# Two small tables placed ahead of hT in on-chip memory, so that hT starts at 192 modulo 512 bytes

## The chip, the core and the metric

The kernel runs on one core of a Trainium2 chip. The core has a matrix engine (TensorE, "PE" in the profile, with its weight loads as "PEld"), a vector engine (VectorE, DVE), a scalar engine (ScalarE, ACT), a general engine (GpSimd, POOL) and a queue that issues transfers (SyncE, SP). Operands lie in on-chip memory of 128 partitions (SBUF); matrix products land in PSUM, a separate memory.

The metric is the device time of one launch in microseconds, the median of several runs. Lower is better.

## What is computed

One layer of a hybrid decoder block on 512 tokens of width 1024, in float32. A single input projection is split into the inputs of a state-space branch, of a dilated attention branch, and of two gates:

```python
h = rms_norm(x, norm_w[layer])
proj = h @ w_in[layer].astype(f32)                 # (512, 1024) @ (1024, 9216)
u_s, z_s, q, k, v, z_a, r_s, r_a = jnp.split(proj, offsets, axis=-1)
y_s = s5_branch(u_s, ...)                          # state-space scan, GELU, GLU with w_glu
y_s = (y_s * jax.nn.silu(z_s)) @ w_ssm_out[layer]
q, k = rms_norm(q, ...), rms_norm(k, ...)          # per head, then partial rotary
y_a = dilated_attention(q, k, v)                   # 3 groups of 8 heads, windows 128/512/2048
y_a = (y_a * jax.nn.silu(z_a)) @ w_attn_out[layer]
m = jax.nn.sigmoid(r_s) * y_s + jax.nn.sigmoid(r_a) * y_a
x = x + m @ w_o[layer]
```

The projection `h @ w_in` is by far the largest product: 9216 of the columns, against 1024 each for `w_glu`, `w_ssm_out`, `w_attn_out` (half as deep) and `w_o`.

## The kernel before, in words

**Split products.** Every float32 operand of a large product is held as two tiles of a reduced float32 format, a high part and a low remainder, and `mm3` (line 122) multiplies hi by hi, hi by lo and lo by hi into the same PSUM bank. So one logical product of a 128-deep slice is three matmuls. In the profile all of these have line L63, the helper that issues a matmul, and are told apart by their tiles: `pj<-hT_hi,w_lo` is a product into the PSUM tile `pj` from `hT_hi` and `w_lo`.

**hT.** The normed input is transposed once, at the start, into `hT_hi` and `hT_lo` (line 220 and 221 allocate them, 250 and 251 write them): 8 slices of 128 channels by 512 tokens, 16,384 bytes per partition each. Every product with `w_in` reads them until about nine tenths of the run. Two kinds of unit do so:

- channel-major units (`cm_unit`, used by `u_unit`, `za_unit`, `zs_unit`, `rs_unit`, `ra_unit`, `v0_unit`): a 128x128 slice of weights is loaded into the array and 512 tokens of hT stream through it. hT is the moving operand. The profile writes such a matmul `pj<-hT_hi,w_hi`.
- token-major units (`wide_granule` for queries, keys and values of one head pair, `tok_granule` with half the width): a 128x128 slice of hT is loaded, and 512 (or 256) columns of weights stream through it. hT is the loaded operand, and the profile writes `pj<-w_hi,hT_hi`: the first name behind the arrow is the moving operand.

The same two kinds of unit run with other activations: `gT` (GELU output, times `w_glu`), `yT` (times `w_ssm_out`) and `aT` (times `w_attn_out`) as moving operands, `mT` (times `w_o`) as the loaded one. So the kernel multiplies in exactly the same shapes with hT and with tiles that lie elsewhere.

**Weights.** `load_w` (line 185) brings a weight tile by SP's queue, splits it with ACT (line 108, `w_hi`) and DVE (line 110, `w_lo`), and has two buffers for the raw tile and three for each part. `get_w` runs two tiles ahead.

**Stages.** Start-up and the first units of `u` (to about 86 us in the profile); the gates and the state-space preparation and scan, interleaved with units that read hT (to about 284 us); `w_glu` and `w_ssm_out` with gT and yT (to 371 us); attention, one head pair after the other, with the next head pair's token-major units between (to about 656 us); `w_attn_out` and `w_o` (to the end).

**Order of work.** A scheduler orders each engine's instructions when the kernel is built. Nothing is reordered at run time except weight loads of TensorE.

**Where tiles lie.** The pool `cst` gives out addresses in the order in which its tiles are allocated, each rounded up to 32 bytes, and gives each its own place for the whole run. It starts with `ident` at byte 16,512 of each partition. `nwc` (the norm weights, 8 numbers, line 207) follows at 17,024, then hT. `wcol` (the query and key norm weights, 6 numbers, line 545) comes far behind, between `maskB` and `tC`. Bytes per partition in the built programs:

```
tile          before            after
nwc           17024             17024
wcol          63136             17056
hT_hi         17056 (160 mod 512)   17088 (192 mod 512)
hT_lo         33440 (160 mod 512)   33472 (192 mod 512)
AT, fT, A4, sza, maskA, maskB     each 32 bytes higher than before
tC, tS and every other pool       where they were
all w_raw, w_hi, w_lo, gT, yT, mT, aT, qkp: 192 mod 512 in both
ident: 128 mod 512 in both
```

Of the kernel before, what the change touches and what calls it, by code (L numbers as in the profile page):

```python
# [11 lines left out]
F32 = mybir.dt.float32  # L12
F32R = mybir.dt.float32r
# [7 lines left out]
P = 128  # L21
D = 1024
S = 512
KT = D // P
# [10 lines left out]
NG = 3  # L35
# [17 lines left out]
def tile_hybrid_block(ctx: ExitStack, tc: tile.TileContext, x, positions, norm_w, w_in, lam_re, lam_im,  # L53
# [21 lines left out]
    cst = ctx.enter_context(tc.tile_pool(name="cst", bufs=1))  # L75
# [24 lines left out]
    def bank(name):  # L100
        return ps_g.tile([P, 512], F32, name=name, tag="g")
# [103 lines left out]
    nw8 = big.tile([KT, P], F32, name="nw8", tag="s7a")  # L205
    act.dma_start(nw8, norm_w[0].rearrange("(k p) -> k p", p=P))
    nwc = cst.tile([P, KT], F32, name="nwc")
    nps = bank("nps")
    pe.transpose(nps[:, 0:KT], nw8, ident[:KT, :KT])
    dve.tensor_copy(nwc, nps[:, 0:KT])  # L210
# [6 lines left out]
        if r in (1, 2):  # L217
            prefetch(len(loaded) + 1)
    lo_w[0] = dve
    hT_hi = cst.tile([P, KT, S], F32R, name="hT_hi")  # L220
    hT_lo = cst.tile([P, KT, S], F32R, name="hT_lo")

    ss = scr([P, NB])
    ms = scr([P, NB])
# [317 lines left out]
    sp.dma_start(qkw[:, 1].rearrange("p g d -> p (g d)"),  # L542
                 k_norm_w[0].rearrange("g d -> (g d)").unsqueeze(0).to_broadcast([P, NG * HD]))
    dve.tensor_scalar(qkw[:, 0], qkw[:, 0], -0.125, None, op0=ALU.mult)
    wcol = cst.tile([P, NG, 2], F32, name="wcol")
    wps = bank("wcp")
    for g in range(NG):
        for a in range(2):
# [633 lines left out]
```

## Time and profile before

| | |
|---|---|
| time, median of 3 runs | 737.64 us (736.49 to 738.57) |
| profiled execution, first to last instruction | 732.6 us |
| median less that span | 5.0 us |
| TensorE busy | 699.6 us (95%), 4821 matmuls |
| VectorE, ScalarE, GpSimd busy | 457.1 us, 314.6 us, 191.7 us |
| transferred | 82.14 MB, mean 112 GB/s |
| granted TensorE clock, mean | 0.993 |

The profile is of one execution; for that one the page gives the span, and no time beside it, so the 5.0 us that lie around it are taken from the median. A busy share counts the time in which at least one instruction is in an engine. Matmuls overlap in the pipeline: one lasts longer than the distance between two starts, so that what a matmul costs in a dense row of them is read from the starts of the first and the last and their count, not from its duration.

### The profile page before, as it was taken

The numbers are of one execution on the slowest core, as the hardware profiler recorded it, in microseconds if no ns is written. First come the engines' busy times: TensorE is split into PE (matmuls) and PEld (weight loads), VectorE is DVE, ScalarE is ACT, GpSimd is POOL, SyncE is SP. The second block draws the span as 40 slices with busy tenths as digits, with TensorE's granted clock in tenths as the row PEclk, the third lists the DMA queues.
The fourth block names the chain that finished last, engine by engine and source line by source line (L and its number), as shares of the span: only waits on it lengthen the run. The fifth ranks groups of instructions, "written<-read, shape, count | busy, mean of one in ns | idle before, by whom it ended". The sixth has DMA issues, their size and how long they took to land.

```text
span 732.6 us, 12680 instructions
## 1 busy us (share of the span) xinstructions
PE 699.6 (95%) x4821; PEld 574.2 (78%) x4821; DVE 457.1 (62%) x912; ACT 314.6 (43%) x631; POOL 191.7 (26%) x346
## 2 busy tenths in 40 slices
PE   2799899999999999999999999999989999999997
PEld 2687688778878787888888888788868877878886
DVE  6759673989946546764335659655664666464832
ACT  6434463332326465442144456537153734443420
POOL 3426540230205343550000316021601250230000
PEclk9999999999999999999999999999999999999999
DMA  8433653564547554455333432222412231326441
GB/s 203 106 96 94 171 144 77 137 149 132 120 131 153 122 103 133 139 168 172 99 100 87 130 87 79 66 58 58 115 31 79 65 89 30 115 73 236 139 144 57
DMA packets 137213, 82.14 MB, mean 112 GB/s; under 512 B 32696, under 2 KB 125632, under 8 KB 137024
## 3 DMA queue, kind: packets, MB, share of 16 engines
q1 hardware_dynamic: 135088, 78.96, 37.5%
q0 software_dynamic: 2048, 2.36, 2.6%
q8 instruction: 38, 0.62, 0.4%
q14 instruction: 23, 0.19, 0.1%
q10 hardware_dynamic: 16, 0.00, 0.0%
HBM read 68.46 MB, written 10.49 MB: 108 GB/s over the span
## 4 chain that ended last, share of the span: by engine, by line
PE 87%; DMA 4%; ACT 3%; DVE 3%; SPq 2%; issue 1%; ACTq 0%
PE pj L63 71%; DMA w_raw<-in_w_in_dram 3%; PE sps L63 3%; PE yps L63 3%; PE ot L63 2%; PE ptp L67 2%; PE kps L63 2%; PE xps L63 1%; PE qtp L67 1%; DMA Uj<-ud 1%; ACT w_hi L108 1%; SPq L442 1%; PE wps L67 1%; ACT qkp L873 1%; DVE w_lo L110 1%
## 5 line engine op out<-in xcount | busy, mean ns | idle before, releaser
L108 ACT ACTIVATE w_hi<-w_raw 128x1024 fp32r<-128x1024 f32 x100 | 106.0, 1061 | 236.8 <-PE pj L63 206.6
L110 DVE TENSOR_TENSOR w_lo<-w_raw,w_hi 128x1024 fp32r<-128x1024 f32 x98 | 124.3, 1268 | 107.9 <-ACT w_hi L108 107.2
L63 PE MATMUL pj<-hT_lo,w_hi 128*128 128x512 f32 (+1 forms) x344 | 132.9, 387 | 3.0 <-DVE hT_lo L251 3.0
L63 PE MATMUL pj<-hT_hi,w_hi 128*128 128x512 f32 (+1 forms) x344 | 132.8, 389 | 2.4 <-ACT V L905 1.4
L63 PE MATMUL pj<-hT_hi,w_lo 128*128 128x512 f32 (+1 forms) x344 | 132.4, 386 | 1.6 <-DVE w_lo L110 1.6
L63 PE MATMUL pj<-w_hi,hT_hi 128*128 128x512 f32 (+1 forms) x288 | 106.5, 372 | 0.0
L63 PE MATMUL pj<-w_lo,hT_hi 128*128 128x512 f32 (+1 forms) x288 | 106.5, 370 | 0.0
L63 PE MATMUL pj<-w_hi,hT_lo 128*128 128x512 f32 (+1 forms) x288 | 106.0, 371 | 0.0
L63 PEld LDWEIGHTS pj<-hT_lo,w_hi 128*128 128x128 f32 x344 | 66.0, 192 | 16.2 <-DVE hT_lo L251 3.9
L63 PEld LDWEIGHTS pj<-hT_hi,w_hi 128*128 128x128 f32 x344 | 65.5, 192 | 16.5 <-ACT V L905 2.1
L63 PEld LDWEIGHTS pj<-hT_hi,w_lo 128*128 128x128 f32 x344 | 65.9, 192 | 15.4 <-DVE w_lo L110 2.3
L63 PEld LDWEIGHTS pj<-w_hi,hT_hi 128*128 128x128 f32 x288 | 54.1, 188 | 10.0 <-issue 0.2
L63 PEld LDWEIGHTS pj<-w_hi,hT_lo 128*128 128x128 f32 x288 | 54.0, 188 | 10.0
L63 PEld LDWEIGHTS pj<-w_lo,hT_hi 128*128 128x128 f32 x288 | 54.0, 188 | 9.8
L931 ACT ACTIVATE Pt<-Pt,st 128x256 f32<-128x256 f32 (+1 forms) x64 | 31.0, 492 | 18.7 <-DVE st L929 18.7
L735 POOL TENSOR_TENSOR kt<-kt,dg 16x128 f32<-16x128 f32 x8 | 4.6, 571 | 125.0 <-ACT kt L734 118.4
L852 POOL TENSOR_TENSOR rt<-qraw,tC 128x256 f32<-128x256 f32 x12 | 14.3, 1189 | 87.7 <-DVE qraw L846 87.4
L739 POOL DMA_DIRECT2D dd<-kt x64 | 33.7, 535 | 2.4 <-POOL kt L735 2.4
L874 DVE SCALAR_TENSOR_TENSOR qkp<-qtp,wcol,qkp 128x512 fp32r<-128x512 f32 (+1 forms) x32 | 23.0, 745 | 13.5 <-ACT qkp L873 13.4
L961 POOL COPY sw<-st 32x4 f32<-32x4 f32 x64 | 12.0, 187 | 73.2 <-ACT Pt L931 70.5
L873 ACT ACTIVATE qkp<-qtp,wcol 128x512 fp32r<-128x512 f32 (+1 forms) x32 | 20.8, 685 | 15.7 <-PE qtp L67 10.4
L277 POOL TENSOR_TENSOR ab<-dd,AT 128x512 f32<-128x512 f32 x16 | 23.0, 1446 | 11.6 <-DVE ab L278 11.6
(263 smaller groups left out, 1289.4 us busy)
## 6 DMA issues: line engine op xcount, KB each, us to landing
w_raw<-in_w_in_dram SPq DMA_DIRECT2D x40, 512.0 KB
w_raw<-in_w_in_dram SPq DMA_DIRECT2D x112, 128.0 KB
w_raw<-in_w_glu_dram SPq DMA_DIRECT2D x8, 512.0 KB
w_raw<-in_w_ssm_out_dram SPq DMA_DIRECT2D x8, 512.0 KB
w_raw<-in_w_o_dram SPq DMA_DIRECT2D x8, 512.0 KB
x_all<-in_x_dram SPq DMA_DIRECT2D x4, 512.0 KB
ud<-uT SPq DMA_DIRECT2D x8, 256.0 KB
Uj<-ud SPq DMA_DIRECT2D x8, 256.0 KB
```

The lines of the kernel that those rows point to most:

```text
L63: last[0] = nc.tensor.matmul(*a, **k)
L67: last[0] = nc.tensor.transpose(*a, **k)
L108: act.activation(hi, src, AF.Copy, scale=scale)
L110: e.tensor_tensor(lo, src, hi.bitcast(F32), op=ALU.subtract)
L277: eng.tensor_tensor(tv, a2.unsqueeze(2).broadcast_to(sh), ai, op=ALU.mult)
L442: sp.dma_start(D1[64 * h:64 * h + 64, a], bv[a][h])
L739: pool.dma_start(M[Q * t:Q * t + Q, :, 0:P - Q * t], kt[:, :, t:].rearrange("q g k p -> q g (k p)"))
L852: pool.tensor_tensor(t1, rh[:, :, :, 0:16], cv.broadcast_to([P, NB * 2, 2, 16]), op=ALU.mult)
L873: act.activation(hi, ps[sl], AF.Copy, scale=w)
L874: dve.scalar_tensor_tensor(lo, ps[sl], w, hi.bitcast(F32), op0=ALU.mult, op1=ALU.subtract)
L931: act.activation(o, o, AF.Exp, bias=nm, scale=-1.0, accum_out=st[:, kind, 1, h, b:b + 1])
L961: pool.tensor_copy(sw[32 * r:32 * r + 32, :, :, b], st[32 * b:32 * b + 32, 1, :, :, r])
```

## The change

`wcol` is allocated right behind `nwc`, and `hT_hi` and `hT_lo` right behind `wcol`, instead of after the loads of x. `wcol` is 24 bytes per partition, which takes 32 in the pool, so hT moves up by 32 bytes, and so does all that lies between hT and the old place of `wcol`.

```diff
     nwc = cst.tile([P, KT], F32, name="nwc")
+    wcol = cst.tile([P, NG, 2], F32, name="wcol")
+    hT_hi = cst.tile([P, KT, S], F32R, name="hT_hi")
+    hT_lo = cst.tile([P, KT, S], F32R, name="hT_lo")
     nps = bank("nps")
...
     lo_w[0] = dve
-    hT_hi = cst.tile([P, KT, S], F32R, name="hT_hi")
-    hT_lo = cst.tile([P, KT, S], F32R, name="hT_lo")
...
     dve.tensor_scalar(qkw[:, 0], qkw[:, 0], -0.125, None, op0=ALU.mult)
-    wcol = cst.tile([P, NG, 2], F32, name="wcol")
     wps = bank("wcp")
```

No instruction is added, removed or moved: on each of the five engines the built programs hold the same instructions in the same order (2677 rows on PE, 777 on DVE, 396 on ACT, 215 on POOL and 152 on SP, equal rows that follow each other counted as one), with the same semaphores; only line numbers and addresses differ.

## The prediction

> **What bounds the kernel now.** I read the page's shares first, then the chain of waits before and after 86 us, then what TensorE waited for.
>
> ```profile
> span 732.6 us, 12680 instructions
> ...
> PE 699.6 (95%) x4821; PEld 574.2 (78%) x4821; DVE 457.1 (62%) x912; ACT 314.6 (43%) x631; POOL 191.7 (26%) x346
> ...
> PE 87%; DMA 4%; ACT 3%; DVE 3%; SPq 2%; issue 1%; ACTq 0%
> ```
>
> The chain that ended last lies on TensorE for 87% of the span. By stretches (0 to 86 us first, then 86 to the end) the same chain reads:
>
> ```profile
> by line: DMA w_raw<-in_w_in_dram 22.1%; PE pj L63 8.8%; DMA Uj<-ud 8.1%; SPq L442 7.9%; DVE w_lo L110 5.2%; SPq L216 5.1%; ACT w_hi L108 4.7%; ACT uT L285 4.1%; issue 4.1%; DVE ab L276 2.7%; DVE hT_lo L251 2.3%; PE wps L67 2.2%; SPq L506 2.
> ...
> by line: PE pj L63 79.7%; PE sps L63 2.9%; PE yps L63 2.9%; PE ot L63 2.4%; PE ptp L67 2.1%; PE kps L63 1.9%; PE xps L63 1.2%; PE qtp L67 1.1%; ACT qkp L873 0.8%; PE wps L67 0.7%; PE cps L63 0.6%; PE yT L67 0.5%; ACT w_hi L108 0.4%; DVE qkp
> ```
>
> So before 86 us transfers and their consumers set the pace, and behind it the large products (`pj`) do. What TensorE waited for behind 86 us, in microseconds in total:
>
> ```profile
> PE qtp L67 <- DVE qkp L874: 3.5, 2, 1.8
> PE pj L63 <- ACT V L905: 1.4, 3, 0.5
> PE pj L63 <- ACT gs L776: 1.0, 1, 1.0
> PE ptp L67 <- DVE qkp L874: 1.0, 2, 0.5
> ```
>
> That is about 7 of 647 us. A matmul that gets cheaper there shortens the run by nearly its whole gain.
>
> **What one matmul costs, by where its operands lie.** No instruction changes, so everything hangs on whether a matmul with hT is dearer than the same one with another tile. Four views of one tile each (`pj`), in dense stretches; a row gives the count, the shortest, median and longest duration in ns, and the starts of the first and last. In order: hT moving; hT loaded; gT and yT moving; mT loaded.
>
> ```profile
> L63 PE MATMUL pj<-hT_hi,w_hi x39: 395/396/397, 152.2 to 178.8; 128*128 128x512 f32 x39
> ```
> ```profile
> L63 PE MATMUL pj<-w_hi,hT_hi x30: 393/396/398, 509.7 to 530.0; 128*128 128x512 f32 x30
> ```
> ```profile
> L63 PE MATMUL pj<-gT_lo,w_hi x64: 389/389/395, 284.5 to 327.4; 128*128 128x512 f32 x64
> ...
> L63 PE MATMUL pj<-yT_lo,w_hi x64: 389/389/389, 328.1 to 370.9; 128*128 128x512 f32 x64
> ```
> ```profile
> L63 PE MATMUL pj<-w_hi,mT_hi x37: 389/389/389, 699.9 to 724.4; 128*128 128x512 f32 x37
> ```
>
> Each logical step is three matmuls, so between the first and last start of a row lie three times (count less one) matmuls.
>
> - hT moving: 26.6 us over 3 x 38 = 114 starts, 233.3 ns each.
> - hT loaded: 20.3 us over 3 x 29 = 87, 233.3 ns.
> - gT and yT moving: 284.5 to 370.9 is 86.4 us over 3 x 127 = 381, 226.8 ns.
> - mT loaded: 24.5 us over 3 x 36 = 108, 226.9 ns.
>
> The durations say the same: 394 to 396 against 389. The shape, the format, the weights' tiles and the clock are the same. The stretches differ in what else runs, but neither value moves with it: the rows of hT moving come from a stretch of gates and those of hT loaded from attention, and both give 233.3. The difference is **6.5 ns, 2.9%**, and it goes with hT, in either role. By the table of addresses hT is the only operand of `pj` that isn't at 192 modulo 512; behind the change it is.
>
> **The change, term by term.** The instructions with hT behind 86 us, by shape (count, then busy us and mean duration, which I don't use):
>
> ```profile
> L63 PE MATMUL pj<-hT_hi,w_lo 128*128 128x512 f32 x255 | 101.9, 400 | 0.0
> L63 PE MATMUL pj<-hT_lo,w_hi 128*128 128x512 f32 x255 | 101.9, 399 | 0.0
> L63 PE MATMUL pj<-hT_hi,w_hi 128*128 128x512 f32 x254 | 101.9, 401 | 1.4 <-ACT V L905 1.4
> L63 PE MATMUL pj<-w_lo,hT_hi 128*128 128x512 f32 x224 | 88.6, 396 | 0.0
> L63 PE MATMUL pj<-w_hi,hT_hi 128*128 128x512 f32 x224 | 88.6, 398 | 0.0
> L63 PE MATMUL pj<-w_hi,hT_lo 128*128 128x512 f32 x224 | 88.1, 397 | 0.0
> L63 PE MATMUL pj<-w_hi,hT_hi 128*128 128x256 f32 x64 | 18.0, 281 | 0.0
> L63 PE MATMUL pj<-w_hi,hT_lo 128*128 128x256 f32 x64 | 17.9, 279 | 0.0
> L63 PE MATMUL pj<-w_lo,hT_hi 128*128 128x256 f32 x64 | 17.9, 279 | 0.0
> ```
>
> 1. *Wide matmuls behind 86 us.* 764 with hT moving, 672 with hT loaded: 1436 x 6.5 ns = **9.3 us**.
> 2. *Half-wide ones.* 192. In the row below they start every 116 ns (10.8 us over 3 x 31 = 93). No row has this shape with all operands at 192. The bounds: nothing saved, or as much as by a wide one, 192 x 6.5 = 1.2 us. I take half of 6.5, since 116 is half of 233.3 and so the cost goes with the columns: **0.6 us**.
>
> ```profile
> L63 PE MATMUL pj<-w_hi,hT_hi x32: 277/279/281, 393.8 to 404.6; 128*128 128x256 f32 x32
> ```
>
> 3. *Before 86 us.* One dense piece of half-wide matmuls is on the chain, 45 of them: 45 x 3.2 = **0.15 us**. The wide ones there, 125 in the three groups below, end in waits for transfers, whose end TensorE doesn't set: I take nothing for them, between 0 and 125 x 6.5 = 0.8 us.
>
> ```profile
> 35.59 7.13 PE pj L63 x45
> ```
> ```profile
> L63 PE MATMUL pj<-hT_hi,w_hi 128*128 128x512 f32 x42 | 17.0, 404 | 0.0
> L63 PE MATMUL pj<-hT_lo,w_hi 128*128 128x512 f32 x42 | 17.0, 404 | 0.0
> L63 PE MATMUL pj<-hT_hi,w_lo 128*128 128x512 f32 x41 | 16.2, 398 | 0.9 <-DVE w_lo L110 0.9
> ```
>
> 4. *What is late next.* The weights must come 2.9% faster in these stretches. The suppliers wait for TensorE rather than the reverse (us in total behind 86 us), and the transfers' share in the stretches with hT is 0.24 to 0.54:
>
> ```profile
> ACT w_hi L108 <- PE pj L63: 200.9, 67, 6.2
> ...
> DVE w_lo L110 <- ACT w_hi L108: 97.5, 52, 6.5
> ```
> ```profile
> 184.00:284.00 100.00, 98.83 (x1355) 80.74 (x1351) 61.73 (x78) 50.08 (x102) 30.92 (x59) 1.00 0.54 126
> ...
> 474.00:600.00 126.00, 123.28 (x654) 99.80 (x655) 77.45 (x216) 58.83 (x146) 36.28 (x89) 1.00 0.24 69
> ```
>
> So they keep up. At the ends of head pairs the chain leaves TensorE for some 5 us of ACT and DVE (here from 601.29 to 606.01), but it comes from TensorE just before, so those microseconds move up with it. The softmax of the last head pair has the thinnest cover: its last scaling runs to 659.8 us, and TensorE is at its first transposes by 659.27. If it didn't move at all, everything gained since the stop at 606 would wait for it, at most 53 us x 2.9% = 1.5 us. But the softmax in turn waits for scores, which TensorE computes between the same matmuls, so most of it follows. I take **0.3 us** off.
>
> ```profile
> 601.29 0.90 ACT w_hi L108
> ...
> 606.01 1.75 PE ptp L67 x7
> ```
> ```profile
> 659.18 0.61 DVE L985 TENSOR_SCALAR Pt<-Pt,sfb 128x256 f32<-128x256 f32 x2
> ...
> 659.27 0.49 PE L67 MATMUL ptp<-ident,Pt 128*128 128x128 f32 x3
> ```
>
> 5. *The other moved tables* (AT, masks, sza and more) are read by DVE, ACT and POOL. DVE shows no price for offset 160: the product that reads AT takes less than one of the same shape that reads only tiles at 192. Nothing, for them and for `wcol`, which stays at 160.
>
> ```profile
> L278 DVE TENSOR_TENSOR ab<-ab 128x576 f32<-128x576 f32 x16 | 12.4, 778 | 0.1
> ...
> L276 DVE TENSOR_TENSOR ab<-p,AT 128x576 f32<-128x576 f32 x16 | 11.9, 754 | 21.8 <-ACT p L707 19.3 <-PE yps L63 2.4
> ```
>
> The sum is 9.3 + 0.6 + 0.15 - 0.3 = 9.8 us. The span goes from 732.6 to 722.8, and with the 5.0 us around it the median of 737.6 goes to **727.8 us**.
>
> 6. *The granted clock.* It was at half speed for some stretches, one of them in the middle of attention:
>
> ```profile
> 36.00:39.00 3.00, 3.00 (x16) 0.50 0.00 0
> ...
> 605.70:609.10 3.40, 3.09 (x13) 0.50 0.31 93
> ```
>
> At half speed 3.4 us do the work of 1.7, so each stretch costs up to 1.7 us. With the stops of TensorE moved up by some microseconds that one may vanish, or one appear at another head pair's end: 1.7 us to either side. By the Trainium skill (TensorE: Matmul & The Clock Gate, "What's actually happening") the window that decides is free-running, so that where it falls would be chance; the trace has the length, and cannot show the rule.
>
> **Rivals.**
>
> - *One role only.* If the offset cost only the moving operand, the loaded case would owe its 233.3 to something else, or the other way round. The gain is 764 x 6.5 = 5.0 or 672 x 6.5 + 0.6 = 5.0 us: 732.6. For it: two different reads cost the same to a tenth of a nanosecond, which is odd. Against it: in the loaded case the moving weights lie at 192, and only hT is left to blame.
> - *The place, not the offset.* hT lies below byte 50,000 and all other large operands above 66,000; if that is the reason, nothing changes: 737.6. No row separates the two. The Trainium skill (SBUF — State Buffer, "Specifications (TRN2)") speaks of cachelines of 16 bytes; 160 and 192 are both multiples of 16, so by that page this change would give nothing, which is this rival's time. The trace does show a price of something about hT, but not yet that 32 bytes remove it.
> - *Same offset, collision.* Behind the change hT and the weights that are read at the same moment start at the same offset. If both reads then fell on the same part of the memory and every matmul with hT lost as much again as it loses now, 9.9 us more: 747.5. It decides from 2.2 us / 1436 = 1.5 ns a matmul, starts above 234.8 ns. Against it: gT, yT and mT have exactly these offsets and run at 226.8.
> - *Another engine takes the gain.* Attention's softmax and splits on DVE and ACT would have to fill a third of it: about 731 us. Against it: the 7 us of waits above.
>
> **How the numbers follow.** The forecast has 0.85, one role 0.04, another engine 0.02, the place 0.06, collision 0.03. About 0.3%, 2.2 us, is what a measurement of this kernel can tell from no change. Faster is 0.85 + 0.04 + 0.02 = 0.91, same 0.06, slower 0.03. The forecast's own range is 9.8 us with up to 0.8 more for the half-wide and early matmuls or 1.2 less for covers, and 1.7 for the clock: 725.3 to 730.7. The range on record reaches on to the one-role case, 725.3 to 732.8, and leaves the place and the collision out.
>
> **What would show it.** Starts of `pj` with hT every 226.7 ns in both roles, medians of 389 ns; half-wide ones at 113.4; gT, yT and mT as they were; the stage from 284 to 371 us of unchanged length but some 3 us earlier; TensorE's waits not above 9 us behind the start. Wrong would be hT at 233.3 still (the place), one of its two roles at 233.3, or 226.7 with waits grown by as much as was saved.

## The result

The changed kernel takes 728.14 us, median of 6 runs (725.61 to 732.08), against 736.26 us for the kernel before in 6 runs on the same footing (734.70 to 738.57). The ratio is 0.9887, with a 95% interval of 0.9863 to 0.9911. In a second comparison it took 728.39 us against 733.92, ratio 0.9917 (0.9887 to 0.9947). So it is faster by about 1%, 6 to 8 us. The forecast was 727.8 us, which holds; the gain was forecast as 9.8 us, and that was too much by 2 to 4 us.

The page of the kernel after, the lines that answer to those shown of before (span, shares, the chain):

```profile
span 726.0 us, 12680 instructions
...
PE 691.6 (95%) x4821; PEld 574.3 (79%) x4821; DVE 455.4 (63%) x912; ACT 314.6 (43%) x631; POOL 190.9 (26%) x346
...
PE 89%; DVE 3%; ACT 2%; SPq 2%; DMA 2%; issue 1%; ACTq 0%
```

The span is 6.6 us shorter and TensorE still carries the chain. This profiled execution took 727.79 us as a whole, 1.8 us more than its span. Another run of the kernel before has the same difference (736.09 us with a span of 734.3). So the 5.0 us that the prediction put around the span of before was mostly a profiled execution that was quicker than the median of the three runs then known.

**The matmuls.** The same views of the tile `pj`, dense stretches, for the kernel after: count, shortest/median/longest duration in ns, first and last start. First hT moving, then hT loaded, each with all three rows of a step.

```profile
L63 PE MATMUL pj<-hT_hi,w_hi x37: 389/389/389, 153.6 to 178.1; 128*128 128x512 f32 x37
L63 PE MATMUL pj<-hT_lo,w_hi x37: 389/389/389, 153.8 to 178.3; 128*128 128x512 f32 x37
```
```profile
L63 PE MATMUL pj<-w_lo,hT_hi x30: 387/389/396, 505.7 to 525.5; 128*128 128x512 f32 x30
L63 PE MATMUL pj<-w_hi,hT_lo x30: 389/389/397, 505.9 to 525.7; 128*128 128x512 f32 x30
L63 PE MATMUL pj<-w_hi,hT_hi x29: 389/389/397, 506.2 to 525.2; 128*128 128x512 f32 x29
```

hT moving: 24.5 us over 3 x 36 = 108 starts is 226.9 ns, where it was 233.3. hT loaded: 89 matmuls from 505.7 to 525.7, 20.0 us over 88 starts, 227.3 ns. The medians are 389 ns in both roles. That is what gT, yT and mT had before, and still have:

```profile
L63 PE MATMUL pj<-gT_hi,w_hi x64: 389/389/504, 282.0 to 325.0; 128*128 128x512 f32 x64
...
L63 PE MATMUL pj<-yT_lo,w_hi x64: 389/389/389, 325.9 to 368.7; 128*128 128x512 f32 x64
```

This stage has kept its length (282.0 to 368.7 here, where the first of gT was at 284.2 and the last of yT at 370.9) and begins 2.2 us earlier. The first matmul with mT was at 684.9 and is at 678.4, 6.5 us earlier. So the gain lies where hT is read, before and behind that stage, and none of it in the stage itself.

**Half-wide matmuls went the other way.** They started every 116 ns. Now (same view, same granule of the program):

```profile
L63 PE MATMUL pj<-w_hi,hT_hi x31: 283/283/283, 391.3 to 402.1; 128*128 128x256 f32 x31
```

10.8 us over 3 x 30 = 90 starts is 120.0 ns, and the duration went from 279 to 283.

**The waits** of TensorE behind the start are what they were, to a tenth of a microsecond (kernel after, from 88 us on):

```profile
PE qtp L67 <- DVE qkp L874: 3.5, 2, 1.8
PE pj L63 <- ACT V L905: 1.4, 3, 0.5
PE pj L63 <- ACT gs L776: 1.0, 1, 1.0
PE ptp L67 <- DVE qkp L874: 1.0, 2, 0.5
```

**The granted clock** cost the profiled execution of after more. Three stretches at half speed of before, 3.4 us each, and then those of after (columns: stretch, its length, TensorE's busy time, clock, transfers):

```profile
35.70:39.10 3.40, 3.40 (x16) 0.50 0.00 0
83.50:86.90 3.40, 3.40 (x22) 0.50 0.58 167
605.70:609.10 3.40, 3.09 (x13) 0.50 0.31 93
```
```profile
33.00:36.60 3.60, 3.15 (x16) 0.53 0.00 0
80.70:87.50 6.80, 4.72 (x43) 0.51 0.69 166
531.30:534.70 3.40, 3.40 (x20) 0.52 0.12 35
```

The one at about 84 us is twice as long, and the one at the end of a head pair's stage has moved from the third head pair's end to the second's. That is 3.4 us more at half speed, worth up to 1.7 us.

### The profile page after: what moved, and what is told of

It is laid out like the page before. It is cut to its first block, busy times and chain, and to the rows that moved or that the text cites. A ratio compares the mean times of both kernels' runs of the same rounds, so it can differ in the third digit from the quotient of the medians.

```text
span 726.0 us, 12680 instructions
## 1 busy us (share of the span) xinstructions
PE 691.6 (95%) x4821; PEld 574.3 (79%) x4821; DVE 455.4 (63%) x912; ACT 314.6 (43%) x631; POOL 190.9 (26%) x346
## 4 chain that ended last, share of the span: by engine, by line
PE 89%; DVE 3%; ACT 2%; SPq 2%; DMA 2%; issue 1%; ACTq 0%
PE pj L63 73%; PE sps L63 3%; PE yps L63 3%; PE ot L63 2%; PE ptp L67 2%; PE kps L63 2%; PE xps L63 1%; DMA Uj<-ud 1%; PE qtp L67 1%; SPq L443 1%; PE wps L67 1%; DVE w_lo L110 1%; DMA w_raw<-in_w_in_dram 1%; ACT qkp L873 1%; SPq L219 1%; ACT w_hi L108 1%
## 5 line engine op out<-in xcount | busy, mean ns | idle before, releaser
L63 PE MATMUL pj<-hT_lo,w_hi 128*128 128x512 f32 (+1 forms) x344 | 130.9, 381 | 3.6 <-DVE hT_lo L252 3.6
L63 PE MATMUL pj<-hT_hi,w_hi 128*128 128x512 f32 (+1 forms) x344 | 130.8, 383 | 2.0 <-ACT V L905 1.4
L63 PE MATMUL pj<-hT_hi,w_lo 128*128 128x512 f32 (+1 forms) x344 | 130.7, 381 | 1.6 <-DVE w_lo L110 1.6
L63 PEld LDWEIGHTS pj<-hT_hi,w_lo 128*128 128x128 f32 x344 | 65.5, 190 | 14.4 <-DVE w_lo L110 2.6
```

Source lines behind the costliest of these rows:

```text
L63: last[0] = nc.tensor.matmul(*a, **k)
```

## The experiments

Two questions were open. First, what makes a matmul dear: where hT lies (its own offset, or its region), that an operand lies off some boundary (theory A), or the distance between the two operands' starts (theory B). Second, the size of the effect for other distances, and whether some distance beats the change.

All kernels below compute the same thing with the same instructions in the same order; they differ in addresses alone, by empty tiles in the pool `cst` or, in one case, by a slice. "Distance" is the start of the moving operand less that of the loaded one, modulo 512 bytes. The start-to-start times in the text are means over all wide matmuls with hT in dense rows of the trace, without the first twelve of a row; the quoted rows show one such row each. In the run with hT split the means are over whole rows, their first matmuls included. Where a kernel ran once, its time alone tells little, since runs of the kernel before lie between 730.8 and 738.7 us; there the reading rests on the start-to-start times.

### Everything behind hT moved along

The kernel before, with hT at 192 and all weights and other activations at 224:

```diff
+    pad0 = cst.tile([P, 8], F32, name="pad0")
     hT_hi = cst.tile([P, KT, S], F32R, name="hT_hi")
     hT_lo = cst.tile([P, KT, S], F32R, name="hT_lo")
```

> hT lies at 192 modulo 512 as in the changed kernel, but through 32 empty bytes ahead of it that move everything behind it too, so that weights, gT, yT, aT and mT lie at 224; wcol is in its old place. Theory A (a matmul is dear when either operand starts off a 64-byte boundary): hT stays at 233.3 ns from start to start because of the weights, and the 672 wide matmuls of gT, yT, aT and mT go from 226.7 to 233.3 ns, 4.4 us more than the kernel before, about 740.7 us. Theory B (dear when the two operands start at different offsets, here 32 bytes apart): hT at 233.3, gT, yT, aT and mT at 226.7, about 736.3 us as before. If only hT's own offset counted: 728 us.

Measured: 735.58 us, beside 734.60 for the kernel before, ratio 1.0012 (0.9983 to 1.0040). hT moving, and gT and yT:

```profile
L63 PE MATMUL pj<-hT_hi,w_hi x31: 395/396/396, 154.9 to 175.9; 128*128 128x512 f32 x31
```
```profile
L63 PE MATMUL pj<-gT_lo,w_hi x64: 389/389/398, 285.6 to 328.4; 128*128 128x512 f32 x64
L63 PE MATMUL pj<-yT_lo,w_hi x64: 389/389/389, 329.1 to 371.9; 128*128 128x512 f32 x64
```

hT is at 192, as in the changed kernel, and yet at 21.0 us / 90 = 233.3 ns. gT and yT, now at 224 with their weights, run at 86.3 us / 381 = 226.5 ns. Theory A falls, and so does hT's own offset. Theory B stands.

### Everything else moved down to hT

The kernel before, with hT left at 160 and in its place, and the pools of weights and activations moved to 160 as well:

```diff
+    pad0 = cst.tile([P, 120], F32, name="pad0")
     tC = cst.tile([P, NG, NB, 2, 16], F32, name="tC")
```

> hT stays at 160 modulo 512 as in the kernel before, and the weights, gT, yT, aT and mT are moved to 160 as well. Theory A (off a 64-byte boundary): all wide matmuls at 233.3 ns, 4.4 us more than the kernel before, about 740.7 us. Theory B (different offsets): all at 226.7 ns, about 728 us.

Measured: 727.95 us, beside 734.60, ratio 0.9902 (0.9867 to 0.9938), the changed kernel's time without moving hT. hT moving:

```profile
L63 PE MATMUL pj<-hT_hi,w_hi x31: 389/389/389, 155.0 to 175.4; 128*128 128x512 f32 x31
```

20.4 us / 90 = 226.7 ns at an address that was dear before. So it is neither hT's place nor its offset. AT, the masks and the other tables lie at 160 here and at 192 in the changed kernel, at the same time within the spread: they cost nothing, as forecast.

### Other distances

Each of these is the changed kernel with p bytes ahead of hT and 512 - p behind it, so that nothing else changes its offset:

```diff
+    pad0 = cst.tile([P, p // 4], F32, name="pad0")
     hT_hi = cst.tile([P, KT, S], F32R, name="hT_hi")
     hT_lo = cst.tile([P, KT, S], F32R, name="hT_lo")
+    pad1 = cst.tile([P, (512 - p) // 4], F32, name="pad1")
```

With p = 32, hT at 224:

> hT lies at 224 modulo 512, all weights and other activations at 192. Theories A and B both expect the cost of the kernel before, 233.3 ns wide and 116.7 ns half-wide, about 736 us; if the price came from 160 in particular, or from hT lying below the weights' offset, it would be 226.7 ns and 728 us.

Measured: 734.65 us, beside 734.60, ratio 0.9997 (0.9971 to 1.0022), 233.3 ns in both roles. 160 was nothing particular.

With p = 64, hT at 256:

> hT lies at 256 modulo 512, all weights and other activations at 192 as before. Theory A (off a 64-byte boundary): 256 is on one, so hT runs at 226.7 ns as in the changed kernel, about 728 us. Theory B (different offsets modulo 512): hT stays at 233.3 ns, about 736 us. Half-wide matmuls tell the same: 120 ns as in the changed kernel by A, 116.7 by B.

Measured: 733.02 us, beside 734.60, ratio 0.9970 (0.9943 to 0.9996). 256 bytes is a rounder address than 192, and it is worse. hT moving, and hT loaded:

```profile
L63 PE MATMUL pj<-hT_hi,w_hi x31: 388/388/388, 155.2 to 175.8; 128*128 128x512 f32 x31
```
```profile
L63 PE MATMUL pj<-w_hi,hT_hi x22: 393/396/398, 374.3 to 389.0; 128*128 128x512 f32 x22
```

20.6 us / 90 = 228.9 ns moving (distance +64), 14.7 us / 63 = 233.3 loaded (distance -64). Theory B had expected the old cost in both roles: the distance has more than two prices, and its sign counts. Half-wide ones with hT loaded took about 113 ns in one piece and 118 in another:

```profile
L63 PE MATMUL pj<-w_hi,hT_hi x15: 276/276/285, 185.4 to 190.2; 128*128 128x256 f32 x15
```
```profile
L63 PE MATMUL pj<-w_hi,hT_hi x25: 281/281/281, 392.5 to 401.0; 128*128 128x256 f32 x25
```

4.8 us over 42 starts is 114 ns by these rounded starts (113.3 behind the first twelve), and 8.5 us over 72 is 118.

With p = 448, hT at 128, one run:

> hT 64 bytes below the offset of the weights (128 against 192). At 64 bytes above, hT moving ran at 229.0 ns and hT loaded at 233.3. If the sign of the distance counts as from the moving operand to the loaded one, the two roles now change places: hT loaded 229, hT moving 233. If it doesn't: the same as at 64 above. About 733 us by either.

Measured: 731.51 us, beside 736.09 for the kernel before. The roles change places, as expected if the sign counts: moving (distance -64) 21.0 us / 90 = 233.3 ns, loaded (distance +64) 14.4 us / 63 = 228.6.

```profile
L63 PE MATMUL pj<-hT_hi,w_hi x31: 393/393/398, 154.7 to 175.7; 128*128 128x512 f32 x31
```
```profile
L63 PE MATMUL pj<-w_hi,hT_hi x22: 388/392/392, 374.3 to 388.7; 128*128 128x512 f32 x22
```

With p = 128 and p = 384, hT at 320 and at 64, one run each:

> hT 128 bytes above the offset of the weights (320 against 192 modulo 512), nothing else moved. The runs before left theory B: what counts is the distance between the starts of the two operands, not where either starts. Theory B64 or B128 (the distance counts modulo 64 or 128): 226.7 ns from start to start, about 728 us; 64 alone is already unlikely, since at a distance of 64 hT as the loaded operand ran at 233.2 ns. Theory B512 (modulo 512): not 226.7 in both roles, 229 to 234 ns, 731 to 736 us.

> hT 128 bytes below the offset of the weights (64 against 192). With a distance that counts modulo 128 or 64: 226.7 ns, about 728 us. With modulo 512: the roles of the run with 128 above change places, 229 to 234 ns, 731 to 736 us.

Measured: 737.09 and 736.00 us. Both roles are at 232.4 to 232.8 ns in both kernels, with medians above the 389 of the cheap case (hT at 320, moving and loaded):

```profile
L63 PE MATMUL pj<-hT_hi,w_hi x28: 392/395/398, 156.9 to 175.8; 128*128 128x512 f32 x28
```
```profile
L63 PE MATMUL pj<-w_hi,hT_hi x22: 390/392/404, 373.8 to 388.5; 128*128 128x512 f32 x22
```

The distance doesn't count modulo 64 or 128.

With p = 256, hT at 448, one run:

> hT 256 bytes above the offset of the weights (448 against 192). If the distance counts modulo 256: 226.7 ns wide and 120 ns half-wide in both roles, about 728 us. If modulo 512, so that the two reads run half a period apart: anything but that, 231 to 234 ns if every distance but zero collides, or less than 226.7 ns if reads half a period apart never meet; each nanosecond on 1436 wide matmuls is 1.4 us.

Measured: 731.87 us in the one run, at a mean granted clock of 0.985 against 0.993 in the profile of before. hT moving, and hT loaded:

```profile
L63 PE MATMUL pj<-hT_lo,w_hi x31: 389/389/389, 154.9 to 175.3; 128*128 128x512 f32 x31
```
```profile
L63 PE MATMUL pj<-w_hi,hT_hi x23: 389/389/389, 373.9 to 388.9; 128*128 128x512 f32 x23
```

20.4 us / 90 = 226.7 ns, and a median of 389 in both roles; half-wide ones at 120.0. A distance of 256 is as good as none, and 128 to either side gives the same price: as far as these distances show it, **the distance counts modulo 256 bytes**. The run's 3.7 us over the changed kernel's median go with the clock. Two stretches of 6.8 us at half speed lie in late attention (a mean of 0.95 over the 140 us below). With those of the start-up, 20.4 us of this run are at half speed, against 13.6 in the profile of the changed kernel, and the 6.8 us more are worth up to 3.4.

```profile
480.00:620.00 140.00, 134.78 (x750) 0.95 0.24 68
```

### 16 bytes

hT at 208, by a slice that starts four numbers into one tile for both parts of hT:

```diff
-    hT_hi = cst.tile([P, KT, S], F32R, name="hT_hi")
-    hT_lo = cst.tile([P, KT, S], F32R, name="hT_lo")
+    hT_all = cst.tile([P, 2 * KT * S + 128], F32R, name="hT_all")
+    hT_hi, hT_lo = (hT_all[:, 4 + i * KT * S:4 + (i + 1) * KT * S].rearrange("p (k s) -> p k s", s=S) for i in range(2))
```

> hT 16 bytes above the offset of the weights (208 against 192). So far distances of 0 and 256 give 226.7 ns, 32 gives 233.3, 64 gives 229 or 233.3 by its sign, 128 gives 232.5. If the two reads are compared in pieces of 32 bytes or more, a distance of 16 is either as zero (226.7 ns, about 728 us) or, where it crosses into the next piece, as 32 (233.3 ns, about 736 us); if single bytes count, something between, about 732 us.

Measured: 735.70 us in one run, beside 733.92. hT moving (distance +16) is at 231.7 ns throughout. hT loaded (distance -16) does both, in different stretches of the same run:

```profile
L63 PE MATMUL pj<-w_lo,hT_all x23: 388/389/390, 373.8 to 388.7; 128*128 128x512 f32 x23
```
```profile
L63 PE MATMUL pj<-w_lo,hT_all x25: 393/395/398, 583.1 to 599.9; 128*128 128x512 f32 x25
```

The first stretch, which follows the dense one of yT, holds 226.7 ns over all its 96 matmuls; this one, which follows a break, holds 233.3 over 90. Both are steady. So at this distance a whole row of matmuls settles into one of two rhythms. What decides between them was not found: two shorter rows of this run, from 489.2 and from 561.0 us, follow a break too and hold 226.7.

### hT_hi at no distance, hT_lo at 32 bytes

The changed kernel with 32 bytes between the two parts of hT (and 480 behind):

```diff
     hT_hi = cst.tile([P, KT, S], F32R, name="hT_hi")
+    pad0 = cst.tile([P, 8], F32, name="pad0")
     hT_lo = cst.tile([P, KT, S], F32R, name="hT_lo")
+    pad1 = cst.tile([P, 120], F32, name="pad1")
```

> hT_hi at 192 modulo 512 like the weights, hT_lo 32 bytes further, at 224. Theory N (the two reads that meet are a matmul's moving operand and the loaded operand of the next matmul, which is read ahead): with hT loaded, the matmul that runs just before one with hT_lo loaded is the dear one, about 233 ns, whatever its own loaded operand; the one with hT_lo itself is cheap when hT_hi comes next. Theory O (a matmul's own two operands): the dear one is the matmul with hT_lo loaded. With hT moving, both expect the matmuls with hT_lo moving to be dear, about 233 ns, and those with hT_hi about 226.7. Time between 728 and 736 us, about 731.

Measured: 732.44 us in one run, beside 733.92. With hT loaded, in a stretch where the order is w_hi by hT_hi, w_lo by hT_hi, w_hi by hT_lo:

```profile
L63 PE MATMUL pj<-w_hi,hT_lo x22: 388/390/395, 373.7 to 388.4; 128*128 128x512 f32 x22
L63 PE MATMUL pj<-w_hi,hT_hi x22: 390/396/397, 373.9 to 388.6; 128*128 128x512 f32 x22
L63 PE MATMUL pj<-w_lo,hT_hi x22: 394/400/401, 374.2 to 388.8; 128*128 128x512 f32 x22
```

The dearest, with a median of 400 ns, is the one whose own two operands are at no distance and whose successor loads hT_lo. The matmul with hT_lo loaded is the cheapest, 390. From start to start the three take 237.8, 229.1 and 232.0 ns over the whole run. That is theory N's order (a matmul streams while the next one's operand is loaded) and speaks against theory O, in one run. But it isn't the whole of it: N had the other two at 226.7, and the three together take 232.9 on average, hardly less than the 233.3 with both parts at a distance. With hT moving it is alike: about 235 ns with hT_lo moving, but 231.4 and 228.4 for the two with hT_hi. It looks as if a disturbed matmul also disturbs its neighbours; how was not shown.

### The changed kernel again

> The changed kernel once more, with more rounds. If the changed kernel's shortfall of some microseconds against the forecast in its profiled execution was one more half-clock stretch, its runs spread by steps of about 1.7 us and follow their granted clocks; the median ratio to the kernel before is 0.987 to 0.991.

Measured: 728.39 us (727.61 to 730.26, 6 runs), ratio 0.9917. Over its two sets of runs the changed kernel's times go with the granted clock of the run: 725.61 and 727.61 us at 0.993, 727.03 to 729.10 at 0.990 and 0.991, 730.26 and 732.08 at 0.985. One 3.4 us stretch at half speed changes the mean clock by 1.7 / 728 = 0.0023, so these look like steps of about one stretch, 1.7 us; the stretches themselves can be counted in the two profiled executions only. The ratio lies just outside the expected range.

## Why the prediction was right, and where it wasn't

**Right: what is bought, and where it is paid.** hT's matmuls went from 233.3 to 226.7 ns in rows of some length, in both roles; the waits didn't grow; the stage of gT and yT kept its length; moved tables cost nothing. Term 4, for covers that turn out too thin, took 0.3 us off, and none of it can be seen in the waits.

**Term 1 was mis-sized.** It took 6.5 ns for each of 1436 matmuls, from long dense rows. Over all matmuls in dense rows behind 86 us, the first ones included, before has 233.2 ns moving and 233.3 loaded, and after 227.9 and 227.5. So the saving is 5.3 ns moving and 5.8 loaded: 764 x 5.3 + 672 x 5.8 = 7.9 us in place of 9.3. What is missing lies at the heads of rows. After a break the first six or so matmuls still take about 231 ns on average, and the row settles then (kernel after, from one break on):

```profile
152.19 0.39 PE L63 MATMUL pj<-hT_hi,w_hi 128*128 128x512 f32 x1
...
153.58 0.39 PE L63 MATMUL pj<-hT_hi,w_hi 128*128 128x512 f32 x1
...
155.62 0.39 PE L63 MATMUL pj<-hT_hi,w_hi 128*128 128x512 f32 x1
```

The first two rows are six matmuls apart, 1.39 us or 232 ns each; the last two nine apart, 2.04 us or 226.7 each. gT, yT and mT, whose rates were taken for hT's, hardly have such breaks.

**Term 2 had the wrong sign.** Half-wide matmuls lost 3.3 ns each instead of gaining them: 192 x 3.3 = 0.6 us lost where 0.6 were to be gained. The step that failed was the scaling of a cost of 233.3 by the columns, and the bounds with it: they went from nothing to a gain and left a loss out, with no row that excluded it.

**Term 3 can't be seen, and term 6 was paid.** At the same matmul, 73.8 us into the execution of before, the profiled execution of after is 0.9 us ahead, and the second profile of the changed kernel 1.4 us behind. At the row of `xps` that starts at 92.4 us in before, they are 0.7 and 1.7 us behind. So the 0.15 us of term 3 are lost in differences of the start-up, and its half-wide piece by itself lost, from 118.3 to 120.0 ns. Both executions of the changed kernel have 3.4 us more at half speed than that of before, all of it ahead of that row: that is term 6, up to 1.7 us. From that row to the end each of the three has one stretch of 3.4 us, and there the changed kernel gains 7.3 and 7.0 us. Terms 1 and 2 as measured give 7.9 - 0.6 = 7.3.

**The range.** It took 0.8 us for upper bounds that by terms 2 and 3 are 0.6 and 0.8, and nothing for the lower bound of term 2, which is 0.6 less. The result doesn't hang on either.

**The baseline.** That 727.8 was nearly met is partly luck: with a gain of 8.1 us from the 737.64 of the three runs then shown the forecast would have been 729.5, and the level of before was 736.26 with six runs, and 734.60 and 733.92 in later sets.

**The rivals.** "The place, not the offset" falls with the result itself, and again with the run that left hT where it was. The Trainium skill (SBUF — State Buffer, "Specifications (TRN2)") has lines of 16 bytes, by which a start at 160 and one at 192 are alike. For the start of hT alone the runs agree: it takes 226.7 ns at 160 as at 192, when the weights start at the same offset. The forecast of no change that was drawn from it failed because the change also moved hT against the weights, by 32 bytes, and that is worth 6.6 ns a matmul. "Same offset, collision" had it the wrong way round for the wide shape, where equal starts are the cheap case; for the half-wide one they are a dear one. "Another engine takes the gain" would have shown in the waits, which are the same to a tenth of a microsecond. "One role only" is wrong for this change, but a distance of 64 bytes does show it, one role at 229 and the other at 233.3.

**What the prediction called the offset is a distance.** It said that hT is the only operand not at 192 modulo 512, which was true, and left open what 192 has to do with it. The runs show: nothing. Two kernels at the same hT address differ by 6.6 ns a matmul, and two at different addresses agree. That a matmul and the load for the next one disturb each other is what the run with hT split at 32 bytes suggests, for it is the matmul ahead of the distant operand that is dearest. The Trainium skill (TensorE: Matmul & The Clock Gate, "Step-by-step: what each phase is for") has two independent read ports, by which loading the next weights takes nothing from the running matmul; the runs here don't fit that, by up to 6.6 ns of 233, if it is the load that disturbs the matmul. What in the memory or the engine makes the two meet, and why the price of a distance is what it is, was not shown and stays open.

## What to carry to other kernels

Before blaming a slow matmul on its shape, compare its start-to-start time with the same shape on other operands in the same trace: here the trace itself held the cheap case. If it is dearer by a few per cent in one tile only, bring the starts of the moving and the loaded operand to the same place modulo 256 bytes, with empty bytes in a pool; an address that is merely round (256 here) doesn't do it. This is shown for matmuls of 512 columns with a new loaded operand each; those of 256 columns lost by it. A rate read from long dense rows is a bound for a kernel of short ones: count the rows' heads apart, and let the bounds of a shape that the trace doesn't show include a loss.

## What the runs showed of the hardware

Wide matmuls (128x512, this format) from start to start, by distance of the moving operand's start from the loaded one's, modulo 256 bytes: 226.7 ns at 0 (found at distances 0 and 256, with hT at 160, 192 and 448); 229 at +64; 231.7 at +16; 233.3 at +32, -32 and -64; 232.4 to 232.8 at 128; and at -16 either 226.7 or 233.3 within one run, steady within a row of some length. Half-wide ones are the reverse: 120.0 ns at 0, and 113.3 to 118.9 in nearly all pieces at the other distances (short pieces at 128 took 120.0 too). So the distance that is best for the wide shape is among the worst for the other. None of the distances tried beats the changed kernel as a whole, and distances between these were not tried.
